# Attention products on all 128 array rows, and values of head pairs in two groups of key blocks

## The chip, the cores and the metric

The kernel runs on one core of a Trainium2 chip. The metric is the device time of one execution in microseconds (us); less is better. All arithmetic is float32, or float32 split into a high and a low part of the faster type fp32r.

## What is computed

Two layers of a hybrid encoder, one inference step, for a prompt of 16 meta tokens and 512 tokens and for eight decode streams of 16 new tokens with 512 cached ones. Each layer is half a feed-forward block, token mixing, half a feed-forward block. Layer 0 mixes by a state space model beside differential attention (4 heads, two maps each), layer 1 by forgetting attention (8 heads of 64) beside latent attention (8 heads, rotary key of 32). Only the attention is touched. Its cores in the reference are these, with masks and biases per kind:

```python
def _masked_softmax_av(s, mask, v):
    p = jax.nn.softmax(jnp.where(mask, s, -jnp.inf), axis=-1)
    return jnp.einsum('bhqk,bkhd->bqhd', p, v.astype(jnp.float32))

def _diff_core(q, k, v, lam, slopes, qpos, qchk, kpos, kchk):
    ...
    p = jax.nn.softmax(jnp.where(mask, s, -jnp.inf), axis=-1)
    w = p[:, :, 0] - lam * p[:, :, 1]
    return jnp.einsum('bhqk,bkhd->bqhd', w, v.astype(jnp.float32))

def _fox_core(q, k, v, fq, fk, qpos, kpos):
    s = jnp.einsum('bqhd,bkhd->bhqk', q, k, preferred_element_type=jnp.float32) * (DH_C ** -0.5)
    s = s + jnp.swapaxes(fq, 1, 2)[..., :, None] - jnp.swapaxes(fk, 1, 2)[..., None, :]
    return _masked_softmax_av(s, kpos[None, :] <= qpos[:, None], v)
```

## The kernel before

The kernel is written with a planner: the code emits instructions for each engine in generators, `weave` interleaves several generators by weights, and the planner then fixes each engine's order by when it expects an instruction's operands and buffers to be ready. Each engine runs its own order strictly. A tile name with `bufs` buffers makes an instruction wait until an older use of the same buffer is over.

Layer 0's attention (`build`, the `run(weave(...))` at L2113) weaves three streams: `rows`, the decode rows of differential attention, nine of them (eight streams and the meta tokens); `heads`, the four prompt heads; and `norms`, the norms of layer 1's cached latent keys, dense products with `wk`. Layer 1's (L2268) weaves `rows` (eight rows of forgetting attention, `mla_absorb`, eight rows of latent attention) with `pairs` (four head pairs of forgetting attention, then four of latent attention). In both, the scores of one head or pair are woven with the values of the one before.

Scores of the prompt (`prompt_scores`, L1260): for a block of 128 queries and all its keys, passes are summed in one bank. `half_chunk` (L830) gives two: the stacked high and low part of the query against the high part of the keys twice over (`kH`, 128 rows), and the high part of the query against the low part of the keys (`kL`, the 64 rows of one half). Forgetting and latent attention add a mask by a product (`tri`, `edge`). VectorE adds the bias and takes the extreme, ScalarE the exponential, VectorE the division.

Values of the prompt (`prompt_pv`, L1287): for each of five key blocks (16 meta keys, then four of 128) `turn` transposes the weights of each head into a bank, VectorE or ScalarE copies them to a tile `pPT`, and L1317 multiplies them with `pv` (`pvm` for the meta block, 16 rows). With one head (`diff_prompt`) the product uses all 128 columns of the array; with a pair, 64 columns for each head. The products of a block are emitted behind the transposes of the next.

Decode rows: `row_scores` (L1177) multiplies four chunks on 32 columns each; `row_values` (L1192) transposes the weights of 528 keys, the last 16 by themselves, and multiplies with the cached values and with `rn`, the 16 new ones (16 array rows). `mla_rows` (L1880) multiplies latent keys on 128 rows and rotary keys `kpt` with `qpe` on 32 rows (partitions 64 to 96), and its new values `vn` on 16 rows. It uses buffers of the pool `at`, which the prompt heads use too. `mla_absorb` (L1752) runs products on 64 rows and is not changed in that.

Loads go through the queue of SyncE (SP), in order: the rows' keys and values (1024 KB each), the prompt values, the rotary keys. GpSimd (POOL) has small additions to the bias rows `nf` (L1471), copies into `rx`, `kpt` and the latent keys.

## Time and profile before

| | us |
|---|---|
| median of three timed runs | 2732.96 |
| lowest and highest | 2726.97, 2735.03 |
| the profiled execution, its own time | 2741.94 |
| its span, first to last instruction | 2739.9 |

The profile is of one execution. PE is TensorE's products, PEld its loads of stationary operands, DVE is VectorE, ACT ScalarE, POOL GpSimd, SP SyncE. `128*64 128x512` in a row of PE is 128 rows and 64 columns of the array and a moving operand of 128 x 512. The ends of PE's instructions are modelled, so how long a pass keeps the array is read from one start to the next and not from its duration. A product of plain f32 leaves two records. PEclk is the granted share of TensorE's full clock of 2.4 GHz; it has two levels, 1.0 and 0.5.

### The profile page before, as it was taken

The numbers are of one execution on the slowest core, as the hardware profiler recorded it, in microseconds if no ns is written. First come the engines' busy times: TensorE is split into PE (matmuls) and PEld (weight loads), VectorE is DVE, ScalarE is ACT, GpSimd is POOL, SyncE is SP. The second block draws the span as 40 slices with busy tenths as digits, with TensorE's granted clock in tenths as the row PEclk, the third lists the DMA queues.
The fourth block names the chain that finished last, engine by engine and source line by source line (L and its number), as shares of the span: only waits on it lengthen the run. The fifth ranks groups of instructions, "written<-read, shape, count | busy, mean of one in ns | idle before, by whom it ended". The sixth has DMA issues, their size and how long they took to land.

```text
span 2739.9 us, 45245 instructions
## 1 busy us (share of the span) xinstructions
PE 2677.4 (98%) x17514; PEld 2443.4 (89%) x17514; DVE 1963.9 (72%) x4012; ACT 1182.6 (43%) x2152; POOL 236.4 (9%) x523
## 2 busy tenths in 40 slices
PE   8999999999999999999999999998999999999999
PEld 8999999877669999999999999986755779999999
DVE  8777877886775866777868677756555666786776
ACT  6434444336443533443534333435443644443333
POOL 1046542130000000000000000002000100000000
PEclk9999999999999999999999999998988999999999
DMA  3233322545633222222222222334464432222222
GB/s 138 81 95 103 96 95 90 194 149 162 240 134 105 80 83 78 79 80 78 74 85 79 80 81 78 126 86 119 128 228 137 128 95 93 80 80 80 85 84 79
DMA packets 130922, 292.22 MB, mean 107 GB/s; under 512 B 29604, under 2 KB 54516, under 8 KB 126420
## 3 DMA queue, kind: packets, MB, share of 16 engines
q1 hardware_dynamic: 128420, 279.26, 32.4%
q0 software_dynamic: 1280, 8.08, 0.7%
q8 instruction: 138, 2.26, 0.4%
q10 hardware_dynamic: 1008, 2.00, 0.2%
q14 instruction: 76, 0.62, 0.1%
HBM read 255.48 MB, written 36.49 MB: 107 GB/s over the span
## 4 chain that ended last, share of the span: by engine, by line
PE 86%; DVE 6%; DMA 3%; ACT 2%; issue 1%; POOL 1%; DVEq 0%; ACTq 0%; SPq 0%; POOLq 0%
PE pa L550 6%; PE pa L551 6%; PE pa L552 6%; PE pd L460 4%; PE pw L460 4%; PE pw L464 4%; PE pw L461 4%; PE pd L461 4%; PE pd L464 4%; PE pc L551 3%; PE pc L550 3%; PE pc L552 3%; PE pmm L330 2%; PE pb L1317 2%; PE pmm L331 2%; PE pmm L332 2%
## 5 line engine op out<-in xcount | busy, mean ns | idle before, releaser
L321 ACT CAST whi<-wraw 128x1024 fp32r<-128x1024 f32 (+4 forms) x426 | 336.2, 790 | 675.9 <-PE pw L461 214.8
L322 DVE TENSOR_TENSOR wlo<-wraw,whi 128x1024 fp32r<-128x1024 f32 (+4 forms) x426 | 385.7, 906 | 136.7 <-ACT whi L321 130.4
L460 PE MATMUL pd<-gh,whi 128*128 128x328 f32 (+1 forms) x704 | 215.4, 313 | 0.5 <-ACT gh L321 0.3
L461 PE MATMUL pw<-gl,whi 128*128 128x328 f32 (+1 forms) x704 | 214.7, 312 | 0.0
L461 PE MATMUL pd<-gl,whi 128*128 128x328 f32 (+1 forms) x704 | 214.3, 312 | 0.0
L460 PE MATMUL pw<-gh,whi 128*128 128x328 f32 (+1 forms) x704 | 214.2, 311 | 0.0
L464 PE MATMUL pd<-gh,wlo 128*128 128x328 f32 (+1 forms) x704 | 162.9, 312 | 0.0
L464 PE MATMUL pw<-gh,wlo 128*128 128x328 f32 (+1 forms) x704 | 161.9, 311 | 0.0
L321 ACT CAST wvh<-wu 128x1024 fp32r<-128x1024 f32 x79 | 83.1, 1051 | 153.6 <-PE pc L551 148.3
L460 PEld LDWEIGHTS pd<-gh,whi 128*128 128x128 f32 x704 | 131.8, 188 | 3.4 <-ACT gh L321 1.4
L460 PEld LDWEIGHTS pw<-gh,whi 128*128 128x128 f32 x704 | 132.2, 188 | 0.2 <-issue 0.2
L461 PEld LDWEIGHTS pd<-gl,whi 128*128 128x128 f32 x704 | 132.0, 188 | 0.3 <-DVE gl L322 0.3
L461 PEld LDWEIGHTS pw<-gl,whi 128*128 128x128 f32 x704 | 132.3, 188 | 0.0
L672 DVE SCALAR_TENSOR_TENSOR mo<-pd,mo 128x328 f32<-128x328 f32 (+1 forms) x120 | 54.0, 492 | 106.2 <-PE pd L464 105.6
L330 PE MATMUL pmm<-whi,hh 128*128 128x512 f32 (+2 forms) x328 | 127.9, 392 | 0.6 <-ACT whi L321 0.4
L331 PE MATMUL pmm<-wlo,hh 128*128 128x512 f32 (+2 forms) x328 | 123.8, 377 | 0.8 <-DVE wlo L322 0.8
L332 PE MATMUL pmm<-whi,hl 128*128 128x512 f32 (+2 forms) x328 | 123.4, 376 | 0.0
L672 DVE SCALAR_TENSOR_TENSOR mo<-pw,mo 128x328 f32<-128x328 f32 (+1 forms) x120 | 54.0, 492 | 95.8 <-PE pw L464 95.7
L464 PEld LDWEIGHTS pd<-gh,wlo 128*128 128x128 f32 x704 | 118.9, 188 | 0.3 <-DVE wlo L322 0.2
L464 PEld LDWEIGHTS pw<-gh,wlo 128*128 128x128 f32 x704 | 118.9, 188 | 0.0
L550 PE MATMUL pa<-ht,wzh 128*128 128x328 f32 (+1 forms) x316 | 99.6, 315 | 7.2 <-ACT u L637 7.2
L857 POOL MEMSET qb<- 128x1152 f32 x2 | 2.1, 1062 | 1167.2 <-DMA X<-mo 1160.3
(652 smaller groups left out, 8177.3 us busy)
## 6 DMA issues: line engine op xcount, KB each, us to landing
wraw<-wi SPq DMA_DIRECT2D x97, 512.0 KB
wu<-wi SPq DMA_DIRECT2D x79, 512.0 KB
wraw<-wo SPq DMA_DIRECT2D x104, 256.0 KB
wraw<-wo SPq DMA_DIRECT2D x48, 320.0 KB
row<-dkT SPq DMA_DIRECT2D x8, 1024.0 KB
wraw<-ckT SPq DMA_DIRECT2D x16, 512.0 KB
row<-dv SPq DMA_DIRECT2D x8, 1024.0 KB
row<-fkT SPq DMA_DIRECT2D x8, 1024.0 KB
```

The costliest lines, as they stand in the source:

```text
L321: nc.scalar.copy(hi, src)
L322: nc.vector.tensor_tensor(lo, src, hi.bitcast(F), op=OP.subtract)
L330: mm(ps, a[0], b[0], start=start, stop=False)
L331: mm(ps, a[0], b[1], start=False, stop=False)
L332: mm(ps, a[1], b[0], start=False, stop=stop)
L460: mm(ps[b], hi[:, ws], xh[:, c], start=start, stop=False)
L461: mm(ps[b], hi[:, ws], xl[:, c], start=False, stop=False)
L464: mm(ps[b], lo[:, ws], xh[:, c], start=False, stop=stop)
L550: nc.tensor.matmul(p[:, A], w[0][:, c], xh, start=start and i == 0, stop=False, skip_group_check=True)
L551: nc.tensor.matmul(p[:, A], w[0][:, c], xl, start=False, stop=False, skip_group_check=True)
L552: nc.tensor.matmul(p[:, A], w[1][:, c], xh, start=False, stop=i == 3, skip_group_check=True)
L672: v.scalar_tensor_tensor(self.x[:, o, c], p[b][:, A], 0.5, self.x[:, o, c], op0=OP.mult, op1=OP.add)
```

## The change

Where a product of attention used fewer than 128 array rows, its operands are padded with zeros to 128: the low keys (`kL` is copied into `kZ`, one tile for each half, by a DMA that GpSimd issues; the other 64 partitions stay zero), the meta values `pvm`, the new values of the decode rows (`vz`, rows 112 to 128, met by the last 128 of the 528 weights), and the rotary part of the latent rows (`kpT` loaded four times, `qpe` zero outside its 32 rows). The products of `prompt_pv` come in two groups, blocks -1 and 0 and blocks 1 to 3, each behind the transposes of its blocks, for pairs; for one head in one group at the end. The decode rows of layer 1 get buffers of their own (`ar`, `rx`, `kraw`, `kpt`). The reciprocals `rk5` are transposed once. Cut to its core:

```diff
         r = slice(64 * hf, 64 * hf + 64)
-        return [(self.qS[:, c, hf], self.kH[:, c, hf]), (self.qS[r, c, hf], self.kL[r, c])]
+        self.nc.gpsimd.dma_start(self.kZ[hf][r], self.kL[r, c])
+        return [(self.qS[:, c, hf], self.kH[:, c, hf]), (self.qS[:, c, hf], self.kZ[hf])]
+    def lo_keys(self, pool):
+        self.kZ = [pool.tile([128, NP], R, name=f"kZ{hf}") for hf in range(2)]
+        for t in self.kZ:
+            self.nc.gpsimd.memset(t.bitcast(F), 0.0)
...
         s = NP + 16 * b if b < 8 else 0
-        vn = at.tile([16, 512], F, name="rn", tag="rn", bufs=2)
-        self.nc.sync.dma_start(vn, self.dram["VN"][s:s + 16])
-        return vn
+        self.nc.sync.dma_start(self.vz[b % 2][112:128], self.dram["VN"][s:s + 16])
+        return self.vz[b % 2]
+    def new_values(self, at):
+        self.vz = [at.tile([128, 512], F, name=f"vz{i}", tag=f"vz{i}", bufs=1) for i in range(2)]
+        for t in self.vz:
+            self.nc.gpsimd.memset(t, 0.0)
...
         x = self.btile()
-        turn(x[:16, :128], S[:, n * 128:n * 128 + 16])
-        nc.scalar.copy(PT[:16, 4], x[:16, :128])
+        turn(x[:, :128], S[:, 400:528])
+        nc.scalar.copy(PT[:, 4], x[:, :128])
         yield
...
                 last = kc == n
-                mm(O[r], PT[:16, 4, r] if last else PT[:, kc, r], vn[:16, w] if last else V[:, kc, w],
-                   start=kc == 0, stop=last)
+                mm(O[r], PT[:, 4 if last else kc, r], vn[:, w] if last else V[:, kc, w], start=kc == 0, stop=last)
         Os = at.tile([128, 128], F, name="Os", tag="Os", bufs=2)
...
             S = at.tile([128, 528], F, name="S", tag="S")
+            if b == 8:
+                nc.gpsimd.memset(S[:, 400:512], 0.0)
             mn = self.sm.tile([128, 1], F, name="mx", tag="mx", bufs=8)
-            nc.vector.tensor_tensor_reduce(S[:, :n], ca["dsamp" if b < 8 else "dmeta"], ps[:, :n], 1.0, 3e38, op0=OP.add,
-                                           op1=OP.min, accum_out=mn)
-            st.update(S=S, Vb=Vb, vn=vn, l=self.exp_rows(S[:, :n], mn))
+            nc.vector.tensor_tensor_reduce(S[:, 528 - n:], ca["dsamp" if b < 8 else "dmeta"], ps[:, :n], 1.0, 3e38,
+                                           op0=OP.add, op1=OP.min, accum_out=mn)
+            st.update(S=S, Vb=Vb, vn=vn, l=self.exp_rows(S[:, 528 - n:], mn))
             yield
...
         nc = self.nc
-        M = 128 // len(Ps)
-        geo = lambda blk: (16 if blk < 0 else 128, 0 if blk < 0 else 16 + 128 * blk, max(blk, 0))
+        n = len(Ps)
+        M = 128 // n
+        geo = lambda blk: (0 if blk < 0 else 16 + 128 * blk, max(blk, 0))
+        PT = {}
         def turn(blk):
-            kr, k0, j0 = geo(blk)
+            k0, j0 = geo(blk)
             w = 512 - 128 * j0
-            PT = []
             for i, P in enumerate(Ps):
...
                 for j in range(j0, 4):
-                    nc.tensor.transpose(pt[:kr, (j - j0) * 128:(j - j0) * 128 + 128], P[j][:, k0:k0 + kr], self.ident)
-                t = at.tile([128, 512], F, name="pPT", tag="pPT", bufs=4)
+                    nc.tensor.transpose(pt[:, (j - j0) * 128:(j - j0) * 128 + 128], P[j][:, k0:k0 + 128], self.ident)
+                if blk < 3:
+                    t = PT[blk, "t", i] = at.tile([128, 512], F, name="pPT", tag="pPT", bufs=4)
+                t = PT[blk, i] = PT[1, "t", i][:, 384:512] if blk == 3 else t[:, :w]
                 if (blk + i) % 2:
-                    nc.scalar.copy(t[:kr, :w], pt[:kr, :w])
+                    nc.scalar.copy(t, pt[:, :w])
                 else:
-                    nc.vector.tensor_copy(t[:kr, :w], pt[:kr, :w])
-                PT.append(t[:kr, :w])
-            return PT
+                    nc.vector.tensor_copy(t, pt[:, :w])
+        def products(blks):
+            for blk in blks:
+                for i in range(n):
+                    nc.tensor.matmul(O[M * i:M * i + M, 128 * geo(blk)[1]:512], V(blk, i), PT[blk, i], start=blk < 0,
+                                     stop=blk == 3)
         yield
-        PT = turn(-1)
-        yield
-        O = self.btile()
-        for blk in range(-1, 4):
-            nxt = turn(blk + 1) if blk < 3 else None
-            for i in range(len(Ps)):
-                nc.tensor.matmul(O[M * i:M * i + M, 128 * geo(blk)[2]:512], V(blk, i), PT[i], start=blk < 0, stop=blk == 3)
-            PT = nxt
-            yield
+        O = None
+        for blks in ((-1, 0), (1, 2, 3)):
+            for blk in blks:
+                turn(blk)
+                yield
+            if n == 2 or blk == 3:
+                O = O or self.btile()
+                products(blks if n == 2 else range(-1, 4))
+                yield
         nc.scalar.copy(dst, O)
...
             nc.vector.tensor_scalar(db, self.ca["dbase"], SLOPES[h], None, op0=OP.mult)
+            hc = [self.half_chunk(h, m) for m in range(2)]
             for j in range(4):
...
                 for m in range(2):
-                    nk, ps, view = self.prompt_scores(self.half_chunk(h, m), j)
+                    nk, ps, view = self.prompt_scores(hc[m], j)
                     if m == 0:
...
         w = slice(128 * c, 128 * c + 128)
...
         self.nc.sync.dma_start(v, src[16:528, w].rearrange("(b p) n -> p b n", p=128))
-        vm = pool.tile([16, 128], F, name="pvm", tag="pvm", bufs=2)
-        self.nc.sync.dma_start(vm, src[0:16, w])
+        vm = pool.tile([128, 128], F, name="pvm", tag="pvm", bufs=2)
+        self.nc.gpsimd.memset(vm, 0.0)
+        self.nc.sync.dma_start(vm[0:16], src[0:16, w])
         n = 128 // heads
...
                 (self.nc.sync if c else self.nc.scalar).dma_start(fb, self.dram["FC"][64 + h, 0:1].to_broadcast([128, 528]))
+                hc = self.half_chunk(c, i)
                 for j in range(4):
-                    nk, ps, view = self.prompt_scores(self.half_chunk(c, i), j, self.triR)
+                    nk, ps, view = self.prompt_scores(hc, j, self.triR)
                     S = at.tile([128, nk], F, name=f"S{j}", tag=f"S{j}", bufs=4)
...
             yield
+        b = self.btile()
+        nc.tensor.transpose(b[:, :128], self.rk5.rearrange("p h q -> p (h q)"), self.ident)
+        nc.scalar.copy(self.rk5T, b[:, :128])
+        for x in self.qpe:
+            nc.gpsimd.memset(x.bitcast(F), 0.0)
         qpe = [x[64:96].rearrange("p b h q -> p h b q") for x in self.qpe]
...
-            rx = at.tile([128, 4, 8, 16], F, name="rx", tag="pPT", bufs=4)
+            rx = vpool.tile([128, 4, 8, 16], F, name="rx", tag="rx", bufs=1)
             r = self.kr[:, 32 * b:32 * b + 32].rearrange("p (a b) -> p a b", a=4)
...
             for kc in range(4):
-                nc.tensor.matmul(pr[:, kc * 128:kc * 128 + 128], rx[:, kc].rearrange("p h q -> p (h q)"), self.ident,
-                                 start=True, stop=True)
+                nc.tensor.transpose(pr[:, kc * 128:kc * 128 + 128], rx[:, kc].rearrange("p h q -> p (h q)"), self.ident)
             rb = at.tile([128, 528], F, name="rb", tag="nf", bufs=2)
             nc.scalar.copy(rb[:, :512], pr)
-            pr = self.btile()
-            nc.tensor.matmul(pr[:, :16], self.rk5.rearrange("p h q -> p (h q)"), self.ident[:, 16 * b:16 * b + 16],
-                             start=True, stop=True)
-            nc.scalar.copy(rb[:, 512:], pr[:, :16])
-            kraw = at.tile([96, 512], F, name="kraw", tag="rn", bufs=2)
-            nc.sync.dma_start(kraw[64:96], self.io["kpT"][:, b])
-            kp = [at.tile([96, 528], R, name=f"kpt{i}", tag="fb", bufs=2) for i in range(2)]
-            self.split(kp[0][64:96, :512], kp[1][64:96, :512], kraw[64:96])
+            nc.gpsimd.tensor_copy(rb[:, 512:], self.rk5T[:, 16 * b:16 * b + 16])
+            kraw = vpool.tile([128, 512], F, name="kraw", tag="kraw", bufs=1)
+            for i in range(4):
+                nc.sync.dma_start(kraw[32 * i:32 * i + 32], self.io["kpT"][:, b])
+            kp = [vpool.tile([128, 528], R, name=f"kpt{i}", tag="kpt", bufs=2) for i in range(2)]
+            self.split(kp[0][:, :512], kp[1][:, :512], kraw)
             for i in range(2):
-                nc.gpsimd.tensor_copy(kp[i][64:96, 512:], self.kp5[i][64:96, 16 * b:16 * b + 16])
+                nc.gpsimd.tensor_copy(kp[i][:, 512:], self.kp5[i][:, 16 * b:16 * b + 16])
             ps = self.mmtile()
...
                              l == 0, False)
-                self.mm3(o, [q[64:96, b].rearrange("p h q -> p (h q)") for q in self.qpe], [x[64:96, w] for x in kp],
-                         False, True)
+                self.mm3(o, [q[:, b].rearrange("p h q -> p (h q)") for q in self.qpe], [x[:, w] for x in kp], False, True)
             S = at.tile([128, 528], F, name="S", tag="S")
...
             nc.sync.dma_start(V.rearrange("p k n -> p (k n)"), self.io["ckn"][b])
-            vn = vpool.tile([16, 256], F, name="vn", tag="vn", bufs=2)
-            nc.sync.dma_start(vn, self.dram["CN"][16 * b:16 * b + 16])
+            vn = self.vz[b % 2]
+            nc.sync.dma_start(vn[112:128, :256], self.dram["CN"][16 * b:16 * b + 16])
             PT = at.tile([128, 5, 128], F, name="rPT", tag="rPT", bufs=2)
...
                 nc.tensor.transpose(pt[:, kc], S[:, kc * 128:kc * 128 + 128], self.ident)
-            nc.tensor.transpose(x[:16, 256:384], S[:, 512:528], self.ident)
+            nc.tensor.transpose(x[:, 256:384], S[:, 400:528], self.ident)
             nc.vector.tensor_copy(PT[:, 0:4], pt)
-            nc.scalar.copy(PT[:16, 4], x[:16, 256:384])
+            nc.scalar.copy(PT[:, 4], x[:, 256:384])
             yield
...
                 nc.tensor.matmul(O, PT[:, kc], V[:, kc], start=kc == 0, stop=False)
-            nc.tensor.matmul(O, PT[:16, 4], vn, start=False, stop=True)
+            nc.tensor.matmul(O, PT[:, 4], vn[:, :256], start=False, stop=True)
             Os = at.tile([128, 256], F, name="Os", tag="Os", bufs=2)
...
     next(norms)
+    k.new_values(at)
+    pool, close_z = k.pool("kz0", Rr)
+    k.lo_keys(pool)
     rp, close_rp = k.pool("rp0", Rr, bufs=2)
...
     close_rp()
+    close_z()
     k.close_rk()
...
     at, close_at = k.pool("at1", Rr, bufs=3)
+    ar, close_ar = k.pool("ar1", Rr, bufs=3)
+    k.new_values(ar)
+    pool, close_z = k.pool("kz1", L)
+    k.lo_keys(pool)
     k.psum(2, 4)
...
         yield from wait(8)
-        yield from stagger(chain(*k.fox_rows(b, at, rp)) for b in range(8))
+        yield from stagger(chain(*k.fox_rows(b, ar, rp)) for b in range(8))
         close_rp()
...
         k.qlat = [k.rk.tile([128, 2, 8, 8, 16], R, name="qlat" + i, tag="row") for i in "hl"]
-        k.qpe = two(pool, [96, 8, 8, 16], "qpe")
+        k.qpe = two(pool, [128, 8, 8, 16], "qpe")
+        k.rk5T = pool.tile([128, 128], F, name="rk5T")
         yield from k.mla_absorb()
...
         olT = two(pool, [128, 2, 8, 128], "olT")
-        yield from stagger(chain(*k.mla_rows(b, at, olT, pool)) for b in range(8))
+        yield from stagger(chain(*k.mla_rows(b, ar, olT, pool)) for b in range(8))
         k.mla_values(olT)
...
     rest.close()
+    close_ar()
     k.drop_first()
...
     k.out_start(sp)
```

## Rows read from the trace of the kernel before

**Rows 1.** The page: busy time of an engine, share of the span, instructions.

```profile
PE   2677.4 (98%) x17514; PEld 2443.4 (89%) x17514; DVE 1963.9 (72%) x4012; ACT 1182.6 (43%) x2152; POOL 236.4 (9%) x523
```

**Rows 2.** Windows of the attention: stretch, length, busy time by engine, PEclk, DMA, GB/s.

```profile
680.00:828.00 148.00, 143.79 (x996) 94.76 (x994) 105.58 (x401) 72.69 (x171) 0.00 (x0) 0.92 0.55 191
1990.00:2095.00 105.00, 101.96 (x736) 54.02 (x735) 57.52 (x230) 39.82 (x109) 2.27 (x9) 0.80 0.61 209
2095.00:2256.00 161.00, 158.46 (x919) 113.63 (x918) 107.18 (x283) 89.46 (x211) 13.31 (x39) 0.96 0.35 109
```

**Rows 3.** Timeline of PE, differential scores: start, us, line, tiles, form, count.

```profile
762.43 0.38 PE L1273 MATMUL pmm<-kL,qS 64*128 64x264 f32 x1
...
763.06 0.38 PE L1273 MATMUL pmm<-kL,qS 64*128 64x264 f32 x1
```

**Rows 4.** Timeline of PE, latent decode row, two passes on 128 rows.

```profile
2168.27 0.28 PE L332 MATMUL pmm<-whi,qlatl 128*128 128x264 f32 x1
2168.39 0.28 PE L330 MATMUL pmm<-whi,qlath 128*128 128x264 f32 x1
```

**Rows 5.** Timeline of PE, forgetting scores at half clock.

```profile
2004.92 0.60 PE L1273 MATMUL pb<-kH,qS 128*128 128x272 f32 x1
2005.45 0.59 PE L1273 MATMUL pb<-kL,qS 64*128 64x272 f32 x1
```

**Rows 6.** Instructions with tile kL: count, duration in ns, first and last start.

```profile
L1273 PE MATMUL pb<-kL,qS x48: 379/426/700, 682.4 to 2098.5; 64*128 64x256 f32 x16, 64*128 64x272 f32 x16, 64*128 64x400 f32 x16
...
L1273 PE MATMUL pmm<-kL,qS x32: 382/385/587, 680.5 to 2091.2; 64*128 64x264 f32 x32
```

**Rows 7.** Timeline of PE, products of the last head pair, four key blocks.

```profile
2246.29 1.08 PE L1317 MATMUL pb<-pPT,pv 128*64 128x512 f32 x4
...
2249.41 0.87 PE L1317 MATMUL pb<-pPT,pv 128*64 128x384 f32 x4
...
2252.38 0.65 PE L1317 MATMUL pb<-pPT,pv 128*64 128x256 f32 x4
...
2254.91 0.44 PE L1317 MATMUL pb<-pPT,pv 128*64 128x128 f32 x4
```

**Rows 8.** Timeline of PE, one key block of an earlier pair.

```profile
2061.80 0.65 PE L1317 MATMUL pb<-pPT,pv 128*64 128x256 f32 x2
...
2063.07 0.65 PE L1317 MATMUL pb<-pPT,pv 128*64 128x256 f32 x2
```

**Rows 9.** Groups by line and form, PE: count, busy us, mean ns, idle before.

```profile
L1317 PE MATMUL pb<-pPT,pv 128*64 128x512 f32 x32 | 16.7, 765 | 0.0
...
L1317 PE MATMUL pb<-pPT,pvm 16*64 16x512 f32 x32 | 11.4, 730 | 0.0
...
L1317 PE MATMUL pb<-pPT,pv 128*64 128x384 f32 x32 | 10.3, 512 | 0.0
...
L1317 PE MATMUL pb<-pPT,pv 128*64 128x256 f32 x32 | 7.1, 405 | 0.0
...
L1317 PE MATMUL pb<-pPT,pv 128*64 128x128 f32 x32 | 5.6, 298 | 0.0
```

**Rows 10.** DMA issues: engine, count, KB each, median us to landing.

```profile
S<-st_tab POOLq DMA_DIRECT2D x16, 493.0 KB, 3.5
```

**Rows 11.** Waits, 1990 to 2260: us in total, times, longest.

```profile
POOL nf L1471 <- DVE dj L1470: 33.0, 4, 15.3
```

**Rows 12.** Timeline of PE, around the rotary passes of a latent row.

```profile
2170.19 0.28 PE L332 MATMUL pmm<-whi,qlatl 128*128 128x264 f32 x1
...
2170.95 0.39 PE L330 MATMUL pmm<-whi,qlath 128*128 128x264 f32 x1
```

**Rows 13.** Two windows of 10 us, columns as in rows 2.

```profile
730.00:740.00 10.00, 9.77 (x87) 7.37 (x86) 7.42 (x29) 4.71 (x12) 0.00 (x0) 1.00 0.88 324
2000.00:2010.00 10.00, 10.00 (x31) 3.73 (x30) 5.15 (x25) 4.91 (x12) 0.00 (x0) 0.50 0.80 256
```

**Rows 14.** The chain that ended last, 680 to 830: start, us, what.

```profile
759.04 9.67 DMA row<-dkT
```

## What the change is predicted to do

> **What bounds the kernel now.** I read the page first: TensorE is busy for 98% of the span [rows 1]. Then the windows over the three stretches that hold the attention [rows 2]: differential attention at 680 to 828 us, forgetting attention at 1990 to 2095, latent attention at 2095 to 2256, 414 us in all. TensorE is busy for 97 to 98% of each, VectorE for 55 to 71%, and TensorE's granted clock is 0.92, 0.80 and 0.96: part of the time runs at the lower of its two levels, 1.2 GHz instead of 2.4. So a nanosecond taken from TensorE here counts, until another engine or a load is late.
>
> "Busy" hides what the change is about; it shows only in start times. In the scores of a prompt head a pass over the high part of the keys (kH, 128 array rows) alternates with one over the low part (kL, 64 array rows). Two such passes of 264 columns, from one kL start to the next, take 0.63 us [rows 3], 0.315 each. Passes of the same 264 columns that stay on all 128 rows, in the decode rows of latent attention, start 0.12 apart [rows 4]. The 0.195 between is the price of each change of shape. At the lower clock a kL pass of 272 columns starts 0.53 after its kH pass [rows 5].
>
> **Part 1, low keys padded to 128 rows.** kL is read by 48 + 32 = 80 passes [rows 6], each behind a kH pass, 40 in either of the first two stretches. Both passes lose their change of shape: 80 x (0.63 - 2 x 0.12) = 31.2 us. The 400-column passes are longer on both sides, so the difference stands. The zero rows themselves cost nothing: the price of 0.12 is already that of 128 rows. What is added: a copy of kL's 64 rows into kZ for each half of each head (16 in all), issued by GpSimd, and two memsets per stretch. The only DMAs that GpSimd issues now are larger (493 KB against 132) and land 3.5 us after issue [rows 10]. kZ has one buffer per half, so a refill waits for that half's last pass, and by the code four score blocks of the other half (forgetting), or a block of the other half with steps of the other streams (differential), come before its next use. I cost refills after the first at nothing; the cover is this other work, if the planner lifts the copy to where the buffer comes free; without it each costs 3.5 and up. The first in each stretch has a memset ahead; it may be exposed for 0 to 5 us, I take 1.5 each, 3 in all.
>
> The copy queues on GpSimd, in order. There a row's small addition to nf has waited 33.0 us in four waits, up to 15.3 [rows 11], and a copy placed behind it would wait too. The padded meta values (pvm) put a GpSimd memset ahead of a load on SP, and on SP the loads of the rows' keys and values queue behind that load. The Trainium skill ("DMA: Bandwidth & Descriptors", section "SWDGE vs HWDGE vs iDMA") adds that a DMA issued by GpSimd has its descriptors written by software, which VectorE can lock out; it would have the copies issued by SP or ScalarE. No row here shows such a lockout, and by the landing time in the row the sum stays as it is.
>
> **Part 2, products of head pairs in two groups.** The values of a head pair use 64 array columns per head, and two heads can run side by side. Where they do, all four records of a key block stand together: 1.08 us for 512 columns, 0.87, 0.65 and 0.44 for the shorter blocks [rows 7]. Often they don't: one head's two records, other work, then the other head's two, 0.65 each at 256 columns [rows 8]. The planner emits each head when its own transposed block has been copied. Summed over the trace the five blocks of the eight pairs are busy for 16.7 + 11.4 + 10.3 + 7.1 + 5.6 = 51.1 us [rows 9]; all side by side they would be 8 x (1.08 + 1.08 + 0.87 + 0.65 + 0.44) = 33.0. Grouped behind their copies, heads and blocks should stand together: 18.1 us. If the planner splits them again, none of it comes. Each pair also enters and leaves the 64-column shape twice instead of five to ten times: with 0.14 per change (next part), 6 to 7 us at most; part is already in the busy sums, I take 4.
>
> **Part 3, the decode rows.** The rotary part of an MLA row's scores uses 32 array rows. From the last full-height pass to the next one behind the three rotary passes it is 0.76 us [rows 12] where four unbroken passes would be 0.48: 0.28 per half, 0.14 per change, 16 halves: 4.5 us. Three further DMAs of kpT per row go on SP, and the split works on 128 partitions instead of 32 at the same length; both lie off the bound. The new keys' values (16 rows to 128) lose one change in 17 rows of the first two attentions and two in 8 MLA rows, the meta values two in 4 heads, and the 16-column product with cmb two in 8 rows: 57 changes at 0.05 to 0.14, 3 to 8 us; I take 5. The reciprocals of the new keys are transposed once instead of eight times: 1 us.
>
> **Sum on TensorE:** 31.2 + 18.1 + 4 + 4.5 + 5 + 1 = 63.8 us: about 19 in the first stretch, 28 in the second, 17 in the third. Against it and for it stand two things.
>
> **Clock.** Low level for the share that [rows 2] give: 2 x (1 - 0.92) x 148 = 24 us, 42 us and 13 us, the last behind passes on 64 rows that don't change. If the first two went, half of 66 us, 33 at most, would come back. The 2000 to 2010 window is wholly at half clock [rows 13] and in it the array alternates kH and kL [rows 5]; with the changes of shape gone the passes are denser. But stretches with other causes remain, such as the wait for a load below. Between 0 and 33, I take 10.
>
> **What is late next.** Forgetting attention moved 209 GB/s x 105 us = 21.9 MB [rows 2]. The best 10 us here reached 324 GB/s [rows 13], and at that rate these bytes need 68 us. The sum would bring the stretch to 105 - 28 - 8 = 69. That is at the floor, and the loads also wait for buffers; I take back 7. In differential attention one key load lay on the chain of waits for 9.67 us [rows 14], there is one buffer for it, and VectorE would reach 106 of about 125 us; I take back 4.
>
> Net: 63.8 + 10 - 7 - 4 - 3 = 60 us. The profiled execution took 2741.94 us (its span 2739.9), 9 above the median 2732.96 of the three timed runs and above the highest of them. Off its own time that is 2682; off the median, which the comparison uses, 2673.
>
> **The rivals.** (a) *The clock comes back wholly.* For it: the lowest mean, 0.80, is where the scores alternate. Then 63.8 + 33 - 3 for the fills = 94, with nothing late: 2639.
> (b) *Loads and VectorE take over.* The order on TensorE is fixed, so a late row load stops everything behind it. For it: 324 GB/s is a peak of one window, the stretch mean is 209. If the second stretch only falls from 105 to 95 us and the others keep two thirds of their 36, it is 10 + 24 - 3 = 31 us: 2702.
> (c) *The kZ refills are exposed; slower.* One place: the first kL pass of each half waits for GpSimd's copy. Sixteen fills with 3.5 us, four of them behind a stuck GpSimd queue at 33.0 / 4 = 8.3 us, are 89 us: 2733 - 60 + 89 = 2762. It decides from 3.8 us per fill on. Against it: GpSimd is busy for 0 and 2.3 us in the first two stretches [rows 2], and the cover above.
> (d) *Half of it doesn't happen.* The planner splits the pairs as before, and some kZ passes get other shapes between them: 63.8 - 22 - 12 - 3 = 27, no regained clock: 2706.
> (e) *Longer runs of transposes lower the clock.* The new groups put 16 and 12 transposes of a pair in a row ahead of products. If each of the eight pairs brought one more stretch at half clock as long as the window in [rows 13], 10 us, then 8 x 5 = 40 us would be lost: 2713. The Trainium skill ("TensorE: Matmul & The Clock Gate", section "Part 4: PE-mode transpose") says that transposes don't count as activity for the clock in the same way; by that rule this happens. Against it: the third stretch holds the transposes and products of four pairs now and has 0.96 [rows 2], and its low clock begins behind other work (next to 64-row passes).
>
> **How the numbers follow.** Forecast 2673 (2655 to 2692): 0.50. (a) 0.14, (b) 0.17, (c) 0.07, (d) 0.07, (e) 0.05. 8 in 10 must take in most of (a), (b) and (d): 2636 (all of the clock, nothing late) to 2710 (no clock, twice what I take back, and the first fills fully exposed: 63.8 - 22 - 10 = 32, with room for (d)). A measurement of this kernel can tell about 0.3%, 8 us, from no change: faster by more than that is all but (c) and part of (e) and (d), 0.88; the same 0.05; slower 0.07.
>
> **What would show it.** Right: kH and kZ passes 0.12 to 0.13 apart at full clock; records of L1317's successor in fours or longer runs, summed near 33 us; granted clock above 0.92 and 0.80 in the first two stretches; these shorter by about 15 and 30 us, the third by about 15, and the feed-forward parts unchanged. Wrong: TensorE idle ahead of kZ passes with the GpSimd copy as releaser (c); idle ahead of row scores on DMA (b); pairs still in twos (d); low clock behind transposes (e). If the passes still start 0.3 apart with 128 rows each, the price is not one of array shape, and Part 1 falls.

## The result and the profile after

| kernel | median, us | lowest to highest | ratio to before, 95% interval |
|---|---|---|---|
| before | 2732.55 | 2726.97 to 2735.03 | |
| after | 2701.32 | 2698.03 to 2706.32 | 0.989 (0.9868 to 0.9912) |

The changed kernel is 31 us faster where 60 were forecast: the sign was right, the size half. Its profiled execution took 2701.16 us, on the median; that of before lies 9 us over its own, so of the 41 us between the two spans (2739.9 and 2699.1) about 10 are not the change. They are in the clock: the granted clock of that execution was 0.981, and in the 27 other executions of this kernel that were run beside the experiments 0.9845 on the mean. What the clock withholds, (1 - granted clock) x span, is 52 us in the one and 42 on the mean of the others.

TensorE's page line and the windows of the three stretches answer [rows 1, 2]; columns as there.

```profile
PE 2610.4 (97%) x17467; PEld 2435.9 (90%) x17467; DVE 1959.4 (73%) x4011; ACT 1179.8 (44%) x2145; POOL 255.3 (9%) x570
680.00:816.00 136.00, 118.92 (x997) 91.40 (x996) 103.34 (x406) 72.28 (x174) 5.71 (x13) 0.94 0.63 212
1979.00:2066.00 87.00, 75.90 (x747) 48.65 (x745) 59.98 (x240) 42.35 (x113) 9.94 (x23) 0.94 0.79 264
2066.00:2216.00 150.00, 140.38 (x869) 113.95 (x869) 102.03 (x273) 85.06 (x200) 14.11 (x51) 0.92 0.41 127
```

TensorE's busy time in the stretches fell from 404.2 to 335.2 us, by 69; its idle time rose from 9.8 to 37.8, by 28. The forecast had 63.8 + 10 on the one side and 14 on the other. Some 9 of the 69 are the clock of the one execution of before; what is left lies under the forecast, and waits twice as long as expected took back half of it.

By stretch, from starts in the timelines: first differential score to first feed-forward product 237.3 us before and 225.6 after (11.7 less); first forgetting score to first absorbing product of the latent rows 110.1 and 87.1 (23.0 less); from there to the last feed-forward part 279.1 and 272.2 (6.9 less). The prediction named about 15, 30 and 15.

Passes of the scores, timeline of PE at the full clock, a block whose keys come in two halves and then one of 256 keys:

```profile
1981.02 0.34 PE L1286 MATMUL pmm<-kH,qS 128*128 128x264 f32 x1
1981.19 0.28 PE L1286 MATMUL pmm<-kZ,qS 128*128 128x264 f32 x1
1981.32 0.29 PE L1286 MATMUL pmm<-kH,qS 128*128 128x264 f32 x1
1981.44 0.28 PE L1286 MATMUL pmm<-kZ,qS 128*128 128x264 f32 x1
...
2008.92 0.36 PE L1286 MATMUL pb<-kH,qS 128*128 128x256 f32 x1
2009.12 0.28 PE L1286 MATMUL pb<-kZ,qS 128*128 128x256 f32 x1
2009.24 0.22 PE L1289 MATMUL pb<-triR,identR 128*128 128x128 f32 x1
```

Within a chain of 128-row passes they stand 0.12 apart, as forecast from [rows 4]. The first kH pass of a block, behind plain f32 transposes or products, still keeps 0.17 to 0.20.

The waits that are new: the start of the first stretch (PE, POOL; then the waits view, us in total, times, longest; then the copies by issue) and of the second.

```profile
685.88 1.02 POOL L840 MEMSET kZ<- 128x528 f32 x2 [8.47 <-issue]
686.84 1.09 POOL L833 DMA_DIRECT2D kZ<-kL  x2
694.60 0.78 PE L1286 MATMUL pb<-kZ,qS 128*128 128x256 f32 x2 [13.37 <-DMA kZ<-kL]
...
PE pb L1286 <- DMA kZ<-kL: 13.4, 1, 13.4
...
kZ<-kL POOLq DMA_DIRECT2D x16, 132.0 KB, 4.5
...
PE pb L1286 <- DVE mx L1546: 5.3, 1, 5.3
DVE S L1546 <- DMA fb<-FC: 6.6, 1, 6.6
```

One fill of 16 is exposed, the first: 13.4 us where 1.5 was taken. The tile lies where the gated unit's pool was and is zeroed only at 685.9; the copy then takes 7.8 us to the first pass. At the start of forgetting attention the scores come 11 us earlier (1979.8 instead of 1991.1) and the load of the bias row fb only 8 (1983.3 instead of 1991.1). Idle time of TensorE grew by 13 us in the first stretch, 8 in the second and 7 in the third.

The windows over the stretches at the lower clock, after and then before (first three columns: stretch, length, TensorE busy):

```profile
683.30:700.40 17.10, 5.73 (x19) 5.04 (x20) 6.87 (x27) 7.34 (x17) 3.08 (x6) 0.50 0.92 290
1987.20:1994.00 6.80, 5.92 (x19) 3.37 (x22) 6.21 (x32) 5.23 (x15) 0.52 (x1) 0.50 0.99 301
2000.90:2004.30 3.40, 3.15 (x15) 2.95 (x15) 2.25 (x8) 1.09 (x3) 0.41 (x2) 0.50 0.97 394
2072.50:2082.70 10.20, 10.20 (x48) 9.24 (x48) 4.08 (x8) 4.68 (x10) 1.40 (x5) 0.50 0.16 42
2099.90:2113.50 13.60, 9.71 (x38) 8.53 (x39) 7.44 (x12) 5.15 (x9) 1.17 (x5) 0.50 0.60 178
sum 51.10, PE 34.72 PEld 29.13 DVE 26.84 ACT 23.49 POOL 6.58; mean PE 6.94 PEld 5.83 DVE 5.37 ACT 4.70 POOL 1.32
```

```profile
683.30:697.00 13.70, 12.08 (x23) 6.22 (x23) 10.01 (x36) 7.45 (x19) 0.00 (x0) 0.50 0.71 249
...
1994.00:2011.10 17.10, 17.10 (x48) 7.46 (x50) 8.54 (x43) 6.16 (x17) 0.00 (x0) 0.50 0.78 254
...
sum 78.50, PE 76.73 PEld 41.53 DVE 40.84 ACT 27.58 POOL 1.51; mean PE 10.96 PEld 5.93 DVE 5.83 ACT 3.94 POOL 0.22
```

Half of the busy time at the lower level is what the clock costs: between these two executions (76.73 - 34.72) / 2 = 21 us came back, where 10 were taken. Over all executions it is less. Their granted clock, and what it withholds on the mean:

| kernel | executions | granted clock, lowest to highest | withheld, us | of it on busy time, us |
|---|---|---|---|---|
| before | 27 | 0.981 to 0.987 | 42 | 39 |
| Part 1 alone | 4 | 0.988 to 0.990 | 29 | 21 |
| Parts 1 and 3 | 4 | 0.983 to 0.989 | 36 | 26 |
| after | 4 | 0.985 to 0.986 | 40 | 30 |
| after, low keys on 64 rows | 10 | 0.979 to 0.983 | 52 | 44 |

The last column is an estimate: withheld time that falls into a wait costs nothing, and each kernel's trace gives the share that falls on busy time (48.5 of 52.1 us before, 30.2 of 40.2 after). So over all executions about 10 us came back.

### The profile page after: what moved, and what is told of

Its sections match the earlier page's. It is cut to its first block, busy times and chain, and to the rows that moved or that the text cites. A ratio compares the mean times of both kernels' runs of the same rounds, so it can differ in the third digit from the quotient of the medians.

```text
span 2699.1 us, 45310 instructions
## 1 busy us (share of the span) xinstructions
PE 2610.4 (97%) x17467; PEld 2435.9 (90%) x17467; DVE 1959.4 (73%) x4011; ACT 1179.8 (44%) x2145; POOL 255.3 (9%) x570
## 3 DMA queue, kind: packets, MB, share of 16 engines
q1 hardware_dynamic: 129572, 280.84, 33.1%
## 4 chain that ended last, share of the span: by engine, by line
PE 81%; DVE 8%; DMA 4%; ACT 3%; issue 2%; POOL 2%; SPq 0%; DVEq 0%; ACTq 0%; POOLq 0%
PE pa L550 6%; PE pa L551 6%; PE pa L552 6%; PE pd L460 4%; PE pw L460 4%; PE pw L464 4%; PE pw L461 4%; PE pd L461 4%; PE pd L464 4%; PE pc L551 3%; PE pc L550 3%; PE pc L552 3%; PE pmm L330 2%; PE pmm L331 2%; PE pmm L332 2%
## 5 line engine op out<-in xcount | busy, mean ns | idle before, releaser
L550 PE MATMUL pa<-hh,whi 128*128 128x328 f32 (+1 forms) x316 | 100.3, 317 | 0.0
```

The source lines that it names most:

```text
L550: nc.tensor.matmul(p[:, A], w[0][:, c], xh, start=start and i == 0, stop=False, skip_group_check=True)
```

## Experiments

The theory: TensorE's saving came from the array shapes, and half of it went into new waits. The rivals: the clock did it, or the pairs; or the waits are not what is missing. For each kernel, its median and ratio, and from its trace: busy time of TensorE in the whole run, what of it the clock cost (half of what is busy at the lower level, whole run), idle time of TensorE from 670 to 2260 us, and work at full clock (busy less what the clock cost). These come from one execution each, and the clock column holds accidents of it: from 1860 to 1900 us, ahead of layer 1's attention, where TensorE's work is the same in all, it ranges from 3 to 10 us.

| kernel | median | ratio, 95% | busy | clock | idle | work |
|---|---|---|---|---|---|---|
| before | 2732.6 | | 2677.4 | 48.5 | 25.5 | 2628.9 |
| Part 1 alone | 2709.3 | 0.9917 (0.9896 to 0.9937) | 2627.5 | 20.6 | 42.3 | 2606.9 |
| Parts 1 and 3 | 2699.6 | 0.9890 (0.9867 to 0.9914) | 2612.1 | 26.8 | 50.7 | 2585.3 |
| after | 2701.3 | 0.9890 (0.9868 to 0.9912) | 2610.4 | 30.2 | 54.9 | 2580.2 |
| after, low keys on 64 rows | 2730.6 | 0.9989 (0.9975 to 1.0004) | 2647.8 | 46.1 | 47.1 | 2601.7 |
| after, pairs together | 2698.1 | 0.9873 (0.9847 to 0.9900) | 2603.2 | 28.8 | 56.8 | 2574.4 |
| after, early bias row | 2694.2 | 0.9867 (0.9843 to 0.9890) | 2605.8 | 27.0 | 52.5 | 2578.8 |
| both of these | 2690.5 | 0.9850 (0.9827 to 0.9874) | 2603.6 | 31.3 | 53.8 | 2572.3 |
| after, first head on 64 rows | 2698.6 | 0.9873 (0.9852 to 0.9895) | 2618.3 | 33.2 | 48.2 | 2585.1 |

**The low keys' array shape by itself.**

```diff
-        return [..., (self.qS[:, c, hf], self.kZ[hf])]
+        return [..., (self.qS[r, c, hf], self.kZ[hf][r])]
```

> The changed kernel, but the pass over the low keys reads only the 64 filled rows of kZ and of the query; copies, zeroing, buffers and all other parts stay. So it isolates the array shape of 80 passes. Theory (a change of array shape costs 0.195 us per pass, 80 x 0.39 = 31.2 us): passes kH to kZ and back 0.3 apart instead of 0.12, TensorE busy 31 us more in the attention, time 20 to 31 us over the changed kernel (some of it lies in waits that it has): 2721 to 2732. Also its low clock in the first two stretches returns in part. Rival (the gain came from the clock and the pairs, the shape costs nothing by itself): at most 5 us over the changed kernel, 2706, and passes 0.12 to 0.15 apart.

2730.58 us, 27 to 29 over the changed kernel: all of the gain is gone. Timeline of PE:

```profile
2036.82 0.36 PE L1286 MATMUL pmm<-kH,qS 128*128 128x264 f32 x1
2037.12 0.39 PE L1286 MATMUL pmm<-kZ,qS 64*128 64x264 f32 x1
2037.43 0.33 PE L1289 MATMUL pmm<-triR,identR 128*128 128x128 f32 x1
```

The passes are 0.30 and 0.31 apart again, with every copy and buffer in place. The theory stands: the price is one of array shape. Of the 29 us, 21.5 are work and 16 the clock (46.1 against 30.2; about 14 over all executions); 8 us less idle time goes against them. Windows of its lower clock in forgetting attention, where after has 6.8 and 3.4 us:

```profile
1997.70:2014.80 17.10, 16.39 (x44) 7.51 (x43) 8.37 (x43) 7.18 (x17) 2.37 (x6) 0.50 0.81 231
2021.60:2028.40 6.80, 6.80 (x57) 4.57 (x57) 4.49 (x18) 3.22 (x9) 0.54 (x1) 0.50 0.36 83
```

**Part 1 alone on the kernel before.** The edits of `half_chunk`, `lo_keys`, `hc` and the kZ pools of the diff shown ahead, and no others.

> The kernel before with Part 1 alone: low keys copied to kZ and read on 128 rows; products of pairs block by block, the decode rows, meta values and rotary keys as before. Theory (all of the time that was gained is Part 1's; the other parts together brought nothing): 26 to 33 us under the kernel before, 2700 to 2707. Rival (Parts 2 and 3 saved some 15 us on TensorE, and the waits for the copies of Part 1 took as much back): Part 1 alone brings 10 to 20 us, 2713 to 2723. In both: wait of 10 to 14 us ahead of the first kZ pass.

2709.3 us, 20 to 23 under before, between the two expectations and nearer to the rival's. Part 1 removes 22 us of work and puts 17 of idle time in their place. Between the two traces it also removes 28 of clock, about 18 over all executions: 22 + 18 - 17 is the 23 measured. All four of its executions have a higher granted clock than any of before. That 64 rows in the changed kernel cost 27 to 29 and Part 1 alone brings 20 to 23 leaves some 6 us for the other parts, and they do more work for it than that (below). The forgetting stretch is done with Part 1: 87.9 us from its first score to the first absorbing product, where the changed kernel has 87.1.

**Products block by block (Parts 1 and 3 without grouping).**

```diff
-        for blks in ((-1, 0), (1, 2, 3)):
-            for blk in blks:
-                turn(blk)
...
+        for blk in range(-1, 4):
+            nxt = turn(blk + 1) if blk < 3 else None
+            for i in range(len(Ps)):
+                nc.tensor.matmul(O[M * i:M * i + M, ...], V(blk, i), PT[i], start=blk < 0, stop=blk == 3)
```

> The changed kernel, but the products of the values are emitted block by block again as before (the products of a block behind the transposes of the next); the meta block stays padded. Theory (grouping has kept the 512-column blocks of the pairs together and saves 51.1 - 43.6 = 7.5 us of their busy time, and their changes of shape): products of the pairs near 50 us busy, time 5 to 12 us over the changed kernel: 2706 to 2713. Rival (grouping has moved nothing that counts, since the products wait for later copies): within 4 us of 2701. Rival of the other side (it held up the array): 4 us or more faster.

2699.6: the rival. The pair products are busy for 46.1 us in it and 43.6 in the changed kernel; grouping is worth 2.5 us of busy time and nothing that can be measured.

**Pairs kept together.**

```diff
-                for i in range(n):
+                for i in reversed(range(n)):
                     nc.tensor.matmul(O[M * i:M * i + M, ...], V(blk, i), PT[blk, i], ...)
```

> The changed kernel with one edit: of each key block the product of the second head of a pair is emitted ahead of that of the first. The second head's transposed block is copied later, so the planner has both ready when it places the first of them, and in TensorE's order the two heads of a block now always stand together. In the changed kernel the blocks of 384 to 128 columns stood apart for most pairs, and the pair products were busy for 43.6 us. Theory (the term of Part 2 was right for pairs that stand together, and only the order kept it from coming): these products near 33 us busy, time 5 to 10 us under the changed kernel's 2701: 2691 to 2696. Rival (a product that waits for the later copy loses what it gains, or the second half of a block's time was already hidden beside other work): busy near 33 us, but time within 4 us of 2701.

Groups by line and form, after and then this kernel (count, busy us, mean ns, idle):

```profile
L1330 PE MATMUL pb<-pPT,pv 128*64 128x384 f32 x32 | 11.2, 512 | 0.0
L1330 PE MATMUL pb<-pPT,pv 128*64 128x512 f32 x32 | 9.7, 598 | 0.0
L1330 PE MATMUL pb<-pPT,pvm 128*64 128x512 f32 x32 | 9.7, 617 | 0.0
L1330 PE MATMUL pb<-pPT,pv 128*64 128x256 f32 x32 | 7.5, 416 | 0.0
L1330 PE MATMUL pb<-pPT,pv 128*64 128x128 f32 x32 | 5.5, 305 | 0.1
```

```profile
L1330 PE MATMUL pb<-pPT,pvm 128*64 128x512 f32 x32 | 8.6, 617 | 0.0
L1330 PE MATMUL pb<-pPT,pv 128*64 128x512 f32 x32 | 8.4, 599 | 0.0
L1330 PE MATMUL pb<-pPT,pv 128*64 128x384 f32 x32 | 6.9, 511 | 0.0
L1330 PE MATMUL pb<-pPT,pv 128*64 128x256 f32 x32 | 5.6, 434 | 0.0
L1330 PE MATMUL pb<-pPT,pv 128*64 128x128 f32 x32 | 3.6, 307 | 0.0
```

43.6 us become 33.1, the sum that the prediction made from [rows 7]; the means per record hardly move, only the overlap of the two heads does. TensorE's busy time in all falls by 7.2, and the time is 3 us lower (2698.08), inside the rival's 4 and not clear of noise. The order was what had kept the pairs apart; most of the 10.5 us is worth little here.

**The first bias rows loaded earlier.**

```diff
-                fb = at.tile([128, 528], F, name="fb", tag="fb", bufs=2)
...
+                fb = at.tile([128, 528], F, name="fb", tag="fb", bufs=2) if c else self.fb0[i]
...
+    raw = k.wp.tile([128, 1056], F, name="wraw", tag="wraw")
+    k.fb0 = [raw[:, 528 * i:528 * i + 528] for i in range(2)]
+    for i in range(2):
+        nc.scalar.dma_start(k.fb0[i], k.dram["FC"][64 + i, 0:1].to_broadcast([128, 528]))
     k.psum(2, 4)
```

> The changed kernel with one edit: the two bias rows fb of the first pair of forgetting attention are loaded into a weight buffer that is free earlier, ahead of the projections' last steps, instead of into the new pool. In the changed kernel TensorE stood idle for 5.3 us at the start of forgetting attention behind VectorE, which waited 6.6 us for that load (3.6 us before the change, since the scores came 11 us later against it). Theory (waits at the starts of the stretches take back the gain): idle there under 1.5 us, 3 to 5 us faster than the changed kernel: 2696 to 2698. Rival (the wait falls into a stretch at half clock and on loads that come next, so that it moves): within 2.5 us of 2701.

Waits of TensorE on the scores' VectorE step in the second stretch, this kernel:

```profile
PE pb L1286 <- DVE mx L1546: 1.2, 2, 1.0
```

5.3 us of waiting become 1.2, and the time falls by 7 (2694.15), more than expected; its four executions all lie below the changed kernel's four. From the first forgetting score to the first absorbing product it is 82.3 us instead of 87.1. Of these 4.8 the load itself gives little: other waits come up, so that TensorE's idle time in the stretch falls only from 10.9 to 9.9, and the clock gives 3.0 (its cost falls from 4.6 to 1.6). The start lies 3 us earlier too, but that arises from 1864 to 1900 us, ahead of the attention, where this trace has 10.2 us at the lower clock and that of after 20.5; the kernel with the pairs together, whose edit lies elsewhere, has 10.2 there too. So the wait went as expected; that the 7 us come from it isn't shown. And since the stretch ends earlier, with no load among the waits of TensorE in it, the sum of its loads at 264 GB/s had not set its end.

**Both together.** 

> The changed kernel with the edits of the two runs beside it: pair products together, and the first bias rows loaded earlier. Theory (both are lost time on the bounding engine): the gains add up to 8 to 15 us: 2686 to 2693. Rival (the loads of forgetting attention set the end of that stretch, 264 GB/s in its windows): no more than 4 us under 2701, and idle time of TensorE on row loads in place of what was saved.

2690.54 us, 39 to 42 under before and 11 under the changed kernel: the sum of the two, as the theory has it. It is the fastest of all kernels here, though its interval (0.9827 to 0.9874) still touches those of each edit alone.

**No copy ahead of the first head.** `half_chunk(0, m)` of the first attention returns the pass on kL's 64 rows; all other heads as after.

> The changed kernel, but the first head of the first attention uses its low keys on 64 array rows as before (10 passes); all else is padded. So no copy stands ahead of the first pass, and the wait of 13.4 us has no cause left. Theory: minus 13.4, plus 10 x 0.39 = 3.9 for the changes of array shape: 9.5 us faster than the changed kernel, about 2692 (2688 to 2696). Rival (the time is lost anyhow to the loads and copies that come next): within 4 us of the changed kernel's 2701, with idle time of TensorE between 690 and 720 us on other waits.

2698.55, 3 us under the changed kernel where 9.5 were expected. The wait of 13.4 us is gone: TensorE is busy for 17.33 us of the first 20, where after has 6.23, and yet the first feed-forward product comes no earlier (907.0 against 905.3 us). Windows of 680 to 700 us, this kernel and then after:

```profile
680.00:700.00 20.00, 17.33 (x72) 10.67 (x70) 13.38 (x44) 12.29 (x26) 2.87 (x8) 0.83 0.88 291
```

```profile
680.00:700.00 20.00, 6.23 (x24) 5.20 (x23) 7.21 (x26) 7.80 (x18) 3.08 (x6) 0.58 0.93 298
```

Where the wait went, from the first score to the first feed-forward product (225.6 us in after, 223.9 here): 9.3 us less idle time, since smaller waits come up; against it 4.5 more work, near the 3.9 that the prediction's price gives for one head on 64 rows, and 3.1 more clock, since work now stands at half clock where the changed kernel has a wait that spends nothing. And the first score starts 3.4 us later, behind products of the gated unit that the planner put first. This execution (2703.77) lies 5 us over the kernel's median, so the median may owe its 3 us to another mix; 3 us are not clear of noise.

**The kZ pool in another place.** The pool `kz0` opens behind `rp0` instead of ahead of it.

> The changed kernel with one edit: the pool of the two padded low-key tiles kZ of the first attention is opened behind the pool of the row values instead of ahead of it, so that it lies over a part of the former gated-unit pool that is read for the last time earlier. In the changed kernel TensorE stood idle for 13.4 us at its first kZ pass: the zeroing began at 685.9 us, only when the last store of that pool had landed. Theory (half of the gain was given back as waits, and this one wait is the largest): zeroing some 5 us earlier, idle ahead of the first kZ pass 3 to 8 us instead of 13.4, the whole 5 to 11 us faster than the changed kernel, 2690 to 2696. Rival (the copy is late because two 1 MB loads share the transfers, its landing took up to 8.1 us, or what is late next takes its place): idle at that pass above 10 us or as much idle right behind it, time within 4 us of the changed kernel's 2701.

2701.57: the rival. The zeroing starts at 684.4 instead of 685.9, since that place too is held by the gated unit (GpSimd stands 5.7 us behind its step `glu_o` on VectorE), and TensorE waits four times for 11.2 us in all (8.6 the longest).

**Copies issued by SP.** `self.nc.sync.dma_start(self.kZ[hf][r].bitcast(F), self.kL[r, c].bitcast(F))`.

> The changed kernel with the copies of kL into kZ issued by SP instead of GpSimd, same bytes. Theory A (a copy issued by GpSimd costs more): landing of 2 to 3 us at the median instead of 4.5, and the first kZ pass waits 9 to 11 us instead of 13.4; but each refill waits for its half's last pass at the head of SP's queue, where the row and weight loads stand behind it, so waits on row loads appear on TensorE: 2700 to 2715 in all. Theory B (the landing is set by what else is moved): landing as with GpSimd, 4 to 8 us, the rest as in A. If no loads are held up and the landing is short, it is faster than the changed kernel, 2695.

2706.5 (0.9908, 0.9893 to 0.9923). Its rows: timeline of SP and PE, then waits of TensorE from 679 to 740 us.

```profile
687.94 1.18 SPq L833 DMA_DIRECT2D kZ<-kL  x2
695.36 0.78 PE L1286 MATMUL pb<-kZ,qS 128*128 128x256 f32 x2 [12.95 <-DMA kZ<-kL]
...
PE pmm L1194 <- DMA row<-dkT: 2.6, 1, 2.6
```

From issue to the first pass 7.4 us, with GpSimd 7.8: theory B. Who issues this first copy matters little to when it can be used, and on SP the row loads queue behind it; the 5 us over the changed kernel are at the edge of the noise. The Trainium skill ("DMA: Bandwidth & Descriptors", section "SWDGE vs HWDGE vs iDMA") has plain copies issued by SP or ScalarE, and a copy into an fp32r tile, which it counts as a cast, by GpSimd alone; so the copy of the changed kernel could move to SP only with both sides read as f32, and here the move brought nothing.

**Row values loaded later.** The two loads `k.ahead["dv", b]` ahead of the first attention left to their rows.

> The changed kernel, but the two 1 MB loads of row values that stood ahead of the first attention come with their rows instead. They were issued at 684.65 us, 2.2 us ahead of the first kZ copies, and the transfers ran at 263 to 333 GB/s while the copy took up to 8.1 us to land. Theory (the copy is long because it shares the transfers with these loads): landing of the first copies near the 2.2 to 4.5 us of the others, wait ahead of the first kZ pass 13.4 down to 8 to 10 us. Rival (it is long by the way GpSimd's copies are written, whatever else is moved): landing 7 to 8 us again. The time can go either way: 2696 to 2706, since row values that come later may be waited for.

2700.34, the wait 13.7 us, landing 8.3 at most. By itself it tells nothing: the planner put the two loads into the same 20 us again, and the transfers ran at 276 GB/s. The trace of the changed kernel tells more, since all 16 copies there have one form and one issuer. The first two land in 7.6 and 8.1 us while 335 to 339 GB/s are moved; the next two, issued 12 us later, land in 2.2 and 2.4 while 87 to 110 GB/s are moved. Beside less than 190 GB/s none takes more than 3.9, and all over 5 us stand beside more than 250. So the landing goes with what else is moved and not with the form; no run takes the loads away to prove it.

**Buffers of the latent rows.** Both edits of the fastest kernel, and `rx` in the buffers pPT as before; then this with the first head on 64 rows.

> The kernel with pair products together and the early bias rows, with one more edit: the spread reciprocals rx of the latent rows lie in the four buffers pPT again, as before the change, instead of in the one buffer that the change gave them. In the changed kernel GpSimd stood for 9.1 and 8.0 us at the copies into rx at the start of the latent rows, behind TensorE's transposes of the previous row and its own order, and the first rotary pass kpt came at 2100.3 us, 33.4 us behind the first absorbing pass; with Part 1 alone these are 23.3 us. Theory (the single buffer of Part 3 ties the rows' start to each other, and TensorE stands idle at half clock there): first rotary pass 5 us or more earlier behind the first absorbing pass, 2 to 5 us faster than the 2690.5 without this edit: 2685 to 2689. Rival (the delay lies in the planner's order and in the loads and splits of kpt, not in rx; or sharing with the pairs costs what it gains): within 2 us of 2690.5, or slower.

> The run beside it, with the first head of the first attention on 64-row low keys as well, so that no copy stands ahead of its first pass. Theory: as between the changed kernel and that edit alone, about 3 us (2698.55 against 2701.32): 2682 to 2687. Rival (that difference was noise: its busy time at half clock and its changes of shape take all of the 13.4 us back): within 1.5 us of the run beside it.

2695.03 (0.987) and 2693.27 (0.9862): no gain over 2690.54. GpSimd's waits at rx fall from 9.1 and 8.0 us to 8.0 and 1.3, but the first rotary pass still stands 36.1 us behind the first absorbing one. So rx is not what holds the rotary pass. The second run is 1.8 us under the first, between the two expectations, and too little to tell.

## Why the prediction was half right

2701 lies outside the 2655 to 2692 that had half of the chances, inside the wide range to 2710, and beside rival (b)'s 2702. Shape was the right mechanism. That the work came to 48.7 of 63.8 us is partly luck: Parts 1 and 2 were too large by 9 and 17, Part 3 too small by 11.

**Part 1 (31.2 us).** Right in kind, too large in size: 22 us of work. The step that was mis-sized is "both passes lose their change of shape: 80 x (0.63 - 2 x 0.12)". It carried the price of two alternating passes ([rows 3]) to all 80, but in most blocks one kH pass stands behind plain f32 work. Over all passes outside the half-clock stretches, mean distance to the next start (cut at 1.2 us; 63 of each before, 71 and 64 after): kH 0.311 before and 0.214 after, low keys 0.330 and 0.156, together 0.27 per pair of passes; times 80 is 22. The first pass of a block gains half.

**Part 2 (18.1 + 4).** The step "grouped behind their copies, heads and blocks should stand together" failed: only the blocks of 512 columns did, since the planner places each head's product when its own copy is ready. The price for togetherness was right (33.1). It had a second error: 51.1 contains time at half clock; with Part 1 alone the same five groups, in the old order, are busy for 46.7 us. And a third: it counted busy time of these products as time of TensorE, where 10.5 us less of the one brought 7.2 of the other. Grouping took 5.1 us of work (2585.3 to 2580.2) and no time that can be measured. Rival (d) said that of the splitting.

**Part 3 (10.5).** Too small. From 670 to 2260 us TensorE changes its array shape 674 times before, 519 with Part 1 alone, 368 with Parts 1 and 3 and 337 after. Part 3 is 151 changes; the prediction counted 89. It left out the transposes into 16 columns, which became 128 columns wide too: 80 of them in the prompt heads, group of before:

```profile
L1301 PE MATMUL pb<-t_c,S 128*16 128x128 f32 x80 | 15.7, 307 | 2.4 <-DVE S L1523 1.4 <-DVE S L1838 1.0
```

151 x 0.14 = 21 us, and the work fell by 21.6. Of this 6 went back in clock and 8 in idle time, most of it at the latent rows: with Part 1 alone the first rotary pass follows the first absorbing one by 23.3 us, with Parts 1 and 3 by 28.4, in the changed kernel by 33.4. "Both lie off the bound", said of the loads of kpT and the split, failed there. First and last start of the loads, Part 1 alone and after:

```profile
L1915 SPq DMA_DIRECT2D kraw<-kpT x7: 311/327/453, 2054.4 to 2127.7; - x7
```

```profile
L1934 SPq DMA_DIRECT2D kraw<-kpT x20: 310/420/439, 2094.8 to 2134.7; - x20
```

The buffers that the change gives them exist 40 us later. That this is the cause wasn't tried, and of the 10 us only half come with the buffers alone.

**Clock (10 of 33).** By the windows above 21 came back: 24 in the first two stretches, less 3 lost in the third. But half of them belong to the one execution of before, and over all executions about 10 are left. That this meets the 10 of the prediction is luck, since it was put between 0 and 33 without a row for the place. Part 1 alone regained about 18, and the other parts lost 8 of them, by the traces 5 at the latent rows. Rival (a) had three times the clock that came back, and "nothing late" was wrong.

**What is late next (14).** 28. The refills after the first cost nothing, as put; rival (c) falls, with one exposed fill of 16. The row loads were not the limit, and rival (b) names 2702 by a mechanism that wasn't there: the forgetting stretch fell to 87.1 us, and to 82.3 with one small load moved. What was missed are starts: the first use of a tile whose place comes free late (13), the first bias row (5) and the first latent rows (7).

**Rival (e)** falls: with products block by block, so without the longer runs of transposes, the third stretch has the same 23.9 us at the lower clock (6.8, 13.7 and 3.4 against 10.2 and 13.7), where Part 1 alone has 10.2. So by these traces something else in Part 3 lowers it there; what, stays open. By the Trainium skill ("TensorE: Matmul & The Clock Gate", section "Part 4: PE-mode transpose") longer runs should have lowered it: this case's traces don't show it.

**The sum as measured:** work 48.7 less, clock 18 less, idle 29 more from 670 to 2260 us: 38 of the 41 us between the spans. With 10 for the clock in place of the 18 of these two executions it is 30, beside the 31 between the medians.

## What to carry to other kernels

Price a change of array shape in the place where it stands, by the distance from one start to the next, and count columns as well as rows; a pass behind plain f32 work gains about half of one between its equals. When work on the bounding engine shrinks, look at the first step of each stretch: a tile whose place is still held, a load that used to be early enough. Where two operations should stand together in a planner's order, emit the one that is ready last first. Before paying for a wait's removal, count what takes its place: removing 13.4 us of waiting at half clock brought about 3, because smaller waits, the old array shape and work at half clock came in. And before a sum of the clock is drawn from two profiled executions, compare their granted clock with that of the other executions: here half of the 18 us were the execution and not the change.

## What was not expected of the hardware

The lower clock follows the 64-row passes: with only their shape put back, 17.1 and 6.8 us at half clock returned at 1997.7 and 2021.6 us, in the place where before has 17.1 and 10.2 and after 6.8 and 3.4. Over all executions no granted clock of a kernel with the 64-row passes reaches that of its pair without them: 0.981 to 0.987 against 0.988 to 0.990, and 0.979 to 0.983 against 0.985 to 0.986. Alternating shapes cost 22 us in work and about 14 to 18 in clock, nearly as much again. And a copy of 132 KB from on-chip memory to on-chip memory took 7.6 to 8.1 us to land while the transfers ran at 335 to 339 GB/s, and 2.2 to 2.4 at 87 to 110 GB/s.
